# The last pass's up layer by seven products of eight, its down layer so in every second group, and two steps of the first pass placed later

## The chip, the cores and the metric

One core of a Trainium2 chip runs the whole kernel. The metric is the device time of one execution in microseconds; of the kernel before there are three runs, and their median is 2684.53 us. TensorE (PE) multiplies matrices out of SBUF into PSUM, which has eight banks here called by number; VectorE (DVE), ScalarE (ACT) and GpSimd (POOL) do the elementwise work; SyncE (SP) issues most of the transfers. Each engine works off its own queue in order.

## The reference

One layer of an encoder on 2048 tokens of width 1024, then a norm. What the change touches is the last third:

```python
h = h + xo @ w_xo[l]                                   # cross-attention, 256 memory tokens

u = rmsnorm(h, norm_mlp_g[l]) @ w_up[l]                # 1024 -> 4096
h = h + jnp.square(jax.nn.relu(u)) @ w_down[l]         # 4096 -> 1024
return rmsnorm(h, norm_final_g)
```

Before it stand a mixer (dilated window attention in eight heads, beside a convolution) with its out-projection, and cross-attention.

## The kernel before

**Passes.** The tokens are worked off in four passes of 512 (`post(p)`, p from 0 to 3; the last is `NG - 1`). A pass does the out-projection, cross-attention in two matrix products (`xs`, the scores; `x`, the probabilities times `bscr`), the norm, the MLP's up layer and its down layer. The attention of pass p + 1 and its convolution are woven into the instructions of pass p by generators, so the last pass runs alone. `first` is the attention of pass 0; its last steps are woven into the out-projection of pass 0.

**Precision.** Every fp32 operand is split into two fp16 halves, a high one (ScalarE copies) and a low one (VectorE subtracts). `mm3` then makes one product of three matmuls: high by high, high by low, low by high.

**The MLP.** The 4096 hidden features are eight groups `fg` of 512. A group has an up layer (1024 x 512 weights, 96 matmuls of 512 columns or as many halves) and a down layer (512 x 1024). In pass 0 the weights are split and stored (`wst`); later passes load the halves. Loaded weights lie in seven rotating tiles (`wtile`).

**Seven products of eight.** A product of matrices in 2 x 2 blocks can be made by seven block products instead of eight, with sums of blocks before and after. `prep` makes the seven weight blocks of the up layer for all eight groups in passes 1 and 2 and stores them (`ust`). `quad` is the up layer of one group by them: the normed tokens are needed as blocks B11, T1, T4, B2 and T32, which `columns` and `put` make in place of the plain halves `y`, and 7 x 24 matmuls of 256 columns run in four steps. In `quad`, `kept` copies a product from PSUM, `done` adds one, multiplies by the norm's factors `rsb`, squares, and splits the result into the halves `hh`. Pass 1 uses `quad` for groups 5 to 7, pass 2 for all, pass 3 for none.

**The last pass before.** `last_mlp` uses the plain up layer (`hidden`, four tiles of 128 features a group). The down layer of groups 0 to 6 is by seven products (`seven`): the raw fp32 weights are loaded as four quarters, VectorE makes four differences of them (`sums` and one more), seven pieces are split into halves (`piece`, a tile of 128 x 1024 each), and `parts` makes the blocks of the hidden features: A11, A12, A22 and the sums S1 to S4. The result is added into rows of tokens (`row`), which `to_rows` turns from columns first. X, Y and Z are pairs of PSUM banks; X takes the products A11, S2, S3 and A22 in turn, and VectorE reads it after each. The last group is plain, and each 128 tokens are normed and written as they are done.

**Order.** The program's order isn't a queue's order. A scheduler orders each engine's queue by a model of times of its own: an instruction goes when it is ready in that model, the earlier one in the program first. `after(...)` and `pinned(...)` hold an instruction behind the last one noted on the same engine. In `combine`, the results of a pair of heads are put together: the loads `ld`, then the sums `csm` (line 1162), the exponentials, the products, a transposition into `cath` and `catl`, which the out-projection needs. In `post`, the norm before the MLP is `rstd_from` (sums on TensorE `nps`, line 1466, then a power on GpSimd and three small steps on VectorE) and `bcast_rows` (four transpositions `nrb`, line 355) into `rsb`.

Of the kernel before, what the change touches and what calls it, by code (L numbers as in the profile page):

```python
# [21 lines left out]
P = 128  # L22
# [26 lines left out]
def hybrid_layer(ctx, tc, A, out):  # L49
# [1576 lines left out]
    def quad(p, fg, src, hh, rsb):  # L1626
# [21 lines left out]
        def done(e, pt, i, z):  # L1648
            DVE.tensor_tensor(e, e, pt, op=ALU.add)
            e3 = halved(e)  # L1650
            last["dve"] = DVE.scalar_tensor_tensor(e3, e3, 0.0, rsb[:, 256 * z:256 * z + 256].unsqueeze(1).to_broadcast([P, 2, 256]),
                                                   op0=ALU.max, op1=ALU.mult)
            ACT.activation(e, e, AF.Square)
            a, b = (t[:, 2 * i:2 * i + 2, 256 * z:256 * z + 256] for t in hh)
            ACT.copy(a, e3)
            DVE.tensor_tensor(b, e3, a, op=ALU.subtract)  # L1656

        X, Y, Z = (ps(f"u{x}", "up") for x in "xyz")
# [16 lines left out]
        Y = ps("uy", "up")  # L1675
# [8 lines left out]
    def post(p):  # L1684
# [10 lines left out]

        y = ytiles("y")
# [36 lines left out]
        for hp in range(XH // 2):  # L1733
# [21 lines left out]
        if p in preps:  # L1755
# [20 lines left out]
        if p == 2:  # L1776
            opened = hidden_tiles(0, order[0])
            opened = (opened, quad(p, order[0], src, opened, rsb))
# [4 lines left out]
        ACT.activation(rsb, rb, AF.Copy, scale=K_UP)  # L1783
# [3 lines left out]
        if p == NG - 1:  # L1787
            last_mlp(hs, y, rsb)
            return
        for g in range(FG // 2):  # L1790
# [3 lines left out]
            for i, fg in enumerate(fgs):  # L1794
# [6 lines left out]
                if src and (p == 2 or fg > 4):  # L1801
                    while fg not in ready:
                        next(prepping[p])
                    yield from main_quad or quad(p, fg, src, ht, rsb)
                    ks = (0, 1, 2, 3, 6, 7, 4, 5)
                    continue
                for c in range(4):
# [9 lines left out]
                    r = tmp("rl")  # L1817
                    last["dve"] = DVE.scalar_tensor_tensor(r, pt, 0.0, rsb, op0=ALU.max, op1=ALU.mult)
                    ACT.activation(r, r, AF.Square)
                    j = 4 * i + c  # L1820
                    last["act"] = ACT.copy(hh["h", j], r)  # L1821
                    DVE.tensor_tensor(hh["l", j], r, hh["h", j], op=ALU.subtract)
# [41 lines left out]
    def last_mlp(hs, y, rsb):  # L1864


        FG, p = 8, NG - 1
        banks.update(up=(4, 5, 6, 7), ux=(0, 1), uy=(2, 3), tr=(0, 1, 2, 3))
        acc = [xp_.tile([P, 4, 512], F32, tag=f"x{q}0", name=f"rows{q}") for q in "hl"]
        grow = [wk.tile([P, 512], F32, tag="sm", name=f"gain_row{c}", bufs=3) for c in range(2)]  # L1870
        for c in range(2):
            dma(grow[c], A["norm_final_g"][512 * c:512 * c + 512].unsqueeze(0).to_broadcast([P, 512]))

# [16 lines left out]
        def hidden(fg, c):  # L1890

            wh, wl = wpost(wcols(w_up, fg * 512 + c * P), f"u{p}{fg}_{c}", S_UP, (P, 8, P), 4 * fg + c, p)
            pt = ps("up", "up")
            for k in range(KC):
                mm3(pt, wh[:, k, :], wl[:, k, :], y["h", k], y["l", k], k == 0, k == KC - 1)
                if fg == 0 and c < 2 and k % 2:
                    to_rows(4 * c + k // 2)
            r = tmp("rl") if c else cv.tile([P, 512], F32, tag="vr", name="rl", bufs=2)
            last["dve"] = DVE.scalar_tensor_tensor(r, pt, 0.0, rsb, op0=ALU.max, op1=ALU.mult)
            ACT.activation(r, r, AF.Square)  # L1900
            return r

        def halves(x):
            return x.rearrange("p (j t) -> p j t", j=2)

        q1 = [xquad(q, 1, f"hq{q}") for q in "hl"]
        z1 = [[zp.tile([P, 512], F16, tag=f"z{3 * i + n}", name=f"hz{i}{n}") for n in range(3)] for i in range(2)]
        A1, S3 = ([halves(x[:, n]) for x in q1] for n in range(2))
        A2 = [x[:, 2:4] for x in q1]
        S12, S4 = [x[0:2] for x in z1], [halves(x[2]) for x in z1]  # L1910

        def parts(rs_, c):
            r, j = rs_[c], c % 2
            lo, hi = r[:, 0:256], r[:, 256:512]
            if c < 2:
                split([x[:, j] for x in A1], lo)
                DVE.tensor_tensor(lo, lo, hi, op=ALU.subtract)
                split([x[:, j] for x in S3], lo)
            else:
                r0 = rs_[j]  # L1920
                split([x[:, j] for x in A2], r)
                DVE.tensor_tensor(r0[:, 256:512], r0[:, 256:512], hi, op=ALU.add)
                DVE.tensor_tensor(r0[:, 0:256], hi, r0[:, 0:256], op=ALU.subtract)
                split([x[j] for x in S12], r0)
                DVE.tensor_tensor(lo, lo, r0[:, 0:256], op=ALU.subtract)
                split([x[:, j] for x in S4], lo)
# [19 lines left out]
        def piece(w, name):  # L1946
            return two(split_to(wtile(name, 4, (P, 2, 512)), w, S_DN))

        def sums(b):

            for o, x, y_ in ((b[0, 0], b[0, 1], b[0, 0]), (b[4], b[1, 1], b[0, 0]), (b[0, 1], b[1, 1], b[0, 1])):
                DVE.tensor_tensor(o, x, y_, op=ALU.subtract)

        def seven(fg, b, first):
            left, right = slice(0, 256), slice(256, 512)
            half = {"A11": A1, "S3": S3, "S4": S4, "A12": [x[:, :, left] for x in A2], "A22": [x[:, :, right] for x in A2]}
            at = {k: (lambda x, j, t, k=k: half[k][x][:, j, P * t:P * t + P]) for k in half}
            at["S2"] = lambda x, j, t: S12[x][j][:, P * t:P * t + P]
            at["S1"] = lambda x, j, t: S12[x][j][:, 256 + P * t:256 + P * t + P]
            X, Y, Z = ([ps(kind, "dn") for _ in range(2)] for kind in ("ux", "uy", "uy"))  # L1960
            for n, (key, w, pts, more, t0, c0) in enumerate((
                    ("A11", b[0, 0], X, False, 0, 0), ("A12", b[1, 0], Y, False, 0, 0),
                    ("S2", b[4], X, True, 0, 1), ("S1", b[0, 0], Z, False, 2, 1),
                    ("S3", b[0, 1], X, True, 2, 1), ("S4", b[1, 1], Z, True, 0, 1),
                    ("A22", b[1, 0], X, True, 2, 0))):
                wh, wl = piece(w, f"d{p}{fg}_{n}") if n else first
                if n == 1:
                    DVE.tensor_tensor(b[1, 0], b[1, 0], b[4], op=ALU.subtract)
                for t in range(2):
# [4 lines left out]
                    last["dve"] = DVE.scalar_tensor_tensor(a, pts[t], K_DN, a, op0=ALU.mult, op1=ALU.add)  # L1974

        rs_ = []
        for fg in range(FG - 1):
            b = {4: room(4, "b")}
            for c in range(4):
                if c or not fg:  # L1980
                    rs_.append(hidden(fg, c))
                for h in range(2) if 0 < c < 3 else ():
                    b[c - 1, h] = quarter(fg, c - 1, h)
                if c == 3:
# [109 lines left out]
```

## Time and profile before

| | us |
|---|---|
| three runs, median (lowest to highest) | 2684.53 (2680.31 to 2685.0) |
| the profiled execution, its own time | 2687.11 |
| its span | 2685.3 |
| its mean granted clock of TensorE | 0.992 |
| bytes read and written in HBM | 376.6 and 131.5 MB |
| last pass, first matmul of the out-projection about | 2222 |
| first matmul of the last pass's up layer | 2357.3 |

A group's row in the profile reads: line, engine, operation, the tile written and those read, their shapes, how many; then busy time, the mean of one in ns, and the idle time of the engine before them with what ended it. A timeline's row begins with start and duration. A row of waits reads: who waited, for whom, total, times, longest.

### The profile page before, as it was taken

The numbers are of one execution on the slowest core, as the hardware profiler recorded it, in microseconds if no ns is written. First come the engines' busy times: TensorE is split into PE (matmuls) and PEld (weight loads), VectorE is DVE, ScalarE is ACT, GpSimd is POOL, SyncE is SP. The second block draws the span as 40 slices with busy tenths as digits, with TensorE's granted clock in tenths as the row PEclk, the third lists the DMA queues.
The fourth block names the chain that finished last, engine by engine and source line by source line (L and its number), as shares of the span: only waits on it lengthen the run. The fifth ranks groups of instructions, "written<-read, shape, count | busy, mean of one in ns | idle before, by whom it ended". The sixth has DMA issues, their size and how long they took to land.

```text
span 2685.3 us, 43789 instructions
## 1 busy us (share of the span) xinstructions
PE 2613.5 (97%) x16786; PEld 1561.7 (58%) x16786; DVE 1982.5 (74%) x3816; ACT 1245.2 (46%) x2189; POOL 226.2 (8%) x285
## 2 busy tenths in 40 slices
PE   8999999999899999999999999999999999999998
PEld 7844448766454555445576676555776565444443
DVE  5886656567679996556799985468999755677976
ACT  5637544476454345334552343256443343443433
POOL 1234002132001011100000000000000000000000
PEclk9999999999999999999999999999999999999999
DMA  9977978665526777855357777454787765323331
GB/s 270 296 259 215 286 227 268 176 194 169 164 85 180 231 218 217 267 183 166 118 161 227 216 233 235 126 159 124 234 272 255 232 227 157 102 71 102 114 114 63
DMA packets 445634, 510.97 MB, mean 190 GB/s; under 512 B 89613, under 2 KB 341441, under 8 KB 444656
## 3 DMA queue, kind: packets, MB, share of 16 engines
q1 hardware_dynamic: 438016, 493.15, 60.1%
q10 hardware_dynamic: 5184, 9.01, 0.9%
q0 software_dynamic: 2224, 6.01, 0.6%
q8 instruction: 132, 2.16, 0.3%
q14 instruction: 78, 0.64, 0.1%
HBM read 376.59 MB, written 131.48 MB: 189 GB/s over the span
## 4 chain that ended last, share of the span: by engine, by line
PE 75%; DVE 12%; DMA 6%; issue 3%; ACT 3%; SPq 1%; POOL 1%; DVEq 0%; POOLq 0%; ACTq 0%
PE dn L376 7%; PE dn L375 7%; PE dn L374 7%; PE up L374 6%; PE up L376 6%; PE up L375 6%; PE lin L376 3%; PE lin L374 3%; PE lin L375 3%; DVE cacc L391 3%; PE xs L375 2%; PE xs L376 2%; PE xs L374 2%; PE pt L1030 2%; PE x L375 2%
## 5 line engine op out<-in xcount | busy, mean ns | idle before, releaser
L391 DVE SCALAR_TENSOR_TENSOR cacc<-cu,cw,cacc 128x512 f32<-128x512 f32 x480 | 365.8, 768 | 5.0
L375 PE MATMUL dn<-hhl,ws_d 128*128 128x512 f16 x768 | 291.6, 380 | 1.4 <-DVE hhl L1656 1.1
L376 PE MATMUL dn<-hhh,ws_d 128*128 128x512 f16 x768 | 291.6, 380 | 0.0
L374 PE MATMUL dn<-hhh,ws_d 128*128 128x512 f16 x768 | 288.9, 380 | 1.0 <-ACT hhh L1821 0.4
L374 PE MATMUL up<-mh,ws_u 128*128 128x512 f16 x512 | 194.1, 380 | 0.9 <-ACT mh L1509 0.9
L375 PE MATMUL up<-ml,ws_u 128*128 128x512 f16 x512 | 194.5, 380 | 0.0
L376 PE MATMUL up<-mh,ws_u 128*128 128x512 f16 x512 | 194.4, 380 | 0.0
L1024 ACT ACTIVATE sm<-sm,o 128x256 f32<-128x256 f32 (+1 forms) x288 | 119.4, 455 | 130.7 <-DVE o L1023 130.2
L1023 DVE CUSTOM_DVE_ANT_0 sm<-s,mask,qks 128x256 f32<-128x256 f32 (+1 forms) x384 | 151.9, 436 | 34.4 <-PE s L1064 33.7
L1034 DVE TENSOR_TENSOR pl<-pt,ph 128x512 f16<-128x512 f32 x160 | 110.1, 688 | 41.2 <-ACT ph L1033 40.5
L1838 DVE SCALAR_TENSOR_TENSOR h<-dn,bd,h 128x512 f32<-128x512 f32 x96 | 71.7, 749 | 78.6 <-PE dn L376 76.9
L376 PEld LDWEIGHTS <-ws_d 128*128 128x128 f16 x768 | 75.3, 98 | 90.9 <-issue 2.1
L1033 ACT CAST ph<-pt 128x512 f16<-128x512 f32 x160 | 91.4, 572 | 77.7 <-PE pt L1030 77.5
L375 PEld LDWEIGHTS <-ws_d 128*128 128x128 f16 x768 | 75.2, 98 | 83.3 <-issue 0.8
L374 PEld LDWEIGHTS <-ws_d 128*128 128x128 f16 x768 | 75.3, 98 | 82.6 <-issue 0.7
L376 PEld LDWEIGHTS <-ws_u 128*128 128x128 f16 x832 | 81.7, 98 | 64.0 <-issue 0.6
L375 PEld LDWEIGHTS <-ws_u 128*128 128x128 f16 x832 | 81.6, 98 | 61.6 <-issue 0.9
L374 PEld LDWEIGHTS <-ws_u 128*128 128x128 f16 x832 | 81.6, 98 | 60.9 <-issue 0.6
L1030 PE MATMUL pt<-ident,sm 128*128 128x128 f32 x640 | 99.4, 277 | 9.0 <-DVE catl L1200 4.2
L376 PE MATMUL o<-cath,ws_o 128*128 128x512 f16 x256 | 97.3, 383 | 4.8 <-DVE ws_o L362 4.8
L1030 PEld LDWEIGHTS pt<-ident,sm 128*128 128x128 f32 x640 | 79.2, 143 | 35.0 <-ACT sm L1024 4.2
L374 PE MATMUL o<-cath,ws_o 128*128 128x512 f16 x256 | 97.3, 382 | 0.8 <-ACT cath L1199 0.7
(556 smaller groups left out, 7296.4 us busy)
## 6 DMA issues: line engine op xcount, KB each, us to landing
ws_t<-ust SPq DMA_DIRECT2D x77, 512.0 KB
ws_d<-wst SPq DMA_DIRECT2D x64, 512.0 KB
ws_u<-wst SPq DMA_DIRECT2D x52, 512.0 KB
ust<-pt SPq DMA_DIRECT2D x48, 512.0 KB
raw_d<-in_w_down_dram SPq DMA_DIRECT2D x36, 512.0 KB
scan<-in_w_up_dram SPq DMA_DIRECT2D x32, 512.0 KB
scan<-in_w_down_dram SPq DMA_DIRECT2D x32, 512.0 KB
raw_o<-in_w_out_dram SPq DMA_DIRECT2D x32, 512.0 KB
```

The costliest lines, as they stand in the source:

```text
L374: PE.matmul(o, lh, rh, start=first, stop=False, skip_group_check=more)
L375: PE.matmul(o, lh, rl, start=False, stop=False, skip_group_check=more)
L376: last["pe"] = PE.matmul(o, ll, rh, start=False, stop=end, skip_group_check=more)
L391: DVE.scalar_tensor_tensor(acc, u[:, t:t + 512], cw[:, c, t:t + 1], acc, op0=ALU.mult, op1=ALU.add)
L1023: last["dve"] = DVE.tensor_tensor_reduce(dst, so, mask[:, 256 * m:256 * m + nk], SCORE, 3e38, ALU.add, ALU.min, mn)
L1024: last["act"] = ACT.activation(dst, dst, AF.Exp, bias=mn, scale=-1.0)
L1030: last["pe"] = PE.transpose(pt[:, j, :], sm[:, j, :], ident)
L1033: ACT.copy(ph, pt)
L1034: DVE.tensor_tensor(pl, pt, ph, op=ALU.subtract)
L1838: last["dve"] = DVE.scalar_tensor_tensor(hs[m], pt, K_DN, hs[m], op0=ALU.mult, op1=ALU.add)
```

## The change

In the last pass, the up layer is made by `quad` in all eight groups, with `ust` as in pass 2; so `columns` and `put` serve pass 3 too. The down layer is by seven products in groups 0, 2, 4 and 6, and plain in groups 1, 3, 5 and 7, with the stored halves of `wst` and matmuls of 256 columns. `quad` takes a `sink` for its results: `into` splits them into `hh` as before, and `blocks` makes A11 to S4 of them.

`last_mlp` becomes a generator that starts with the pass: it loads the quarters of group 0 at the head of the pass, makes their differences and first four pieces during the scores of the second pair of heads, and starts the first `quad` ahead of the norm. The pieces of a group by seven products lie in four tiles of the pool of `cath` and `catl`, are made ahead one step after each tile of the plain group before it (`steps_ahead`), and the last three inside `seven`. Each group's down layer runs behind the first step of the next group's up layer.

In pass 0, the combination of the last pair starts three empty steps later. In passes 0 and 1, `norm` runs in two parts behind the first and second tile of the up layer, and these two tiles are finished together.

```diff
@@ combine
         if end:
             ld = lds[p, pr]
+            for _ in range(3):
+                yield
@@ post
+        env = {}
+        mlp = last_mlp(hs, env) if p == NG - 1 else None
+        if mlp:
+            next(mlp)
...
                         late.append((pth, ptl, t, soft(sps[t], t)))
+                if mlp and hp:
+                    next(mlp)
                 yield
...
-        if p in preps:
+        if p:
             one, two_, src = columns(p)
...
-        r = rstd_from(ssum)
-        rb = ps("c", "nrb")
-        bcast_rows(rb, r, 4)
-        ACT.activation(rsb, rb, AF.Copy, scale=K_UP)
+        elif mlp:
+            env.update(src=src, rsb=rsb)
+            next(mlp)
+
+        def norm(step, st={}):
+
+            if step == 0:
+                st[0] = rstd_from(ssum)
+            elif step == 1:
+                rb = ps("c", "nrb")
+                bcast_rows(rb, st[0], 4)
+                ACT.activation(rsb, rb, AF.Copy, scale=K_UP)
+
+        held = None if p > 1 else []
+        if held is None:
+            norm(0)
+            norm(1)
...
+                    if held is None:
+                        finish(pt, 4 * i + c)
+                    else:
+                        norm(len(held))
+                        held.append((pt, c))
+                        if len(held) == 2:
+                            for a in held:
+                                finish(*a)
+                            held = None
@@ last_mlp
+            def sink(e, i, z):
+                q[i, z] = e
+                if z == i or i:
+                    split({(0, 0): A1, (1, 1): A22, (1, 0): A12}[i, z], halved(e))
+                    return
+                DVE.tensor_tensor(q[0, 0], q[0, 0], e, op=ALU.subtract)
+                DVE.tensor_tensor(e, e, q[1, 1], op=ALU.add)
+                DVE.tensor_tensor(q[1, 1], q[1, 1], q[0, 0], op=ALU.subtract)
+                split(S2, halved(q[1, 1]))
+                split(S1, halved(e))
+                DVE.tensor_tensor(q[1, 0], q[1, 0], q[1, 1], op=ALU.subtract)
+                split(S3, halved(q[0, 0]))
+                split(S4, halved(q[1, 0]))
...
+            q = [piece(n, w) for n, w in enumerate(((0, 0), (1, 0), 4, (0, 0), (0, 1), (1, 1), (1, 0)))]
+            return [q[0], sub((0, 0), (0, 1), (0, 0)), sub(4, (1, 1), (0, 0)), sub((0, 1), (1, 1), (0, 1)), q[1],
+                    sub((1, 0), (1, 0), 4), q[2], q[3]], q[4:]
...
+        def plain(fg, todo):
+
+            ws = [wpost(wcols(w_down, m * 256, 256, (4 * fg, 4 * fg + 4)), f"d{p}{fg}_{m}", S_DN, (P, 4, 256),
+                        32 + 4 * fg + m, p) for m in range(4)]
+            for t in range(4):
+                for c in range(2):
+                    pt = ps("tr", "dn")
+                    for h in range(2):
+                        wh, wl = ws[2 * c + h]
+                        for k in range(4):
+                            mm3(halved(pt)[:, h], *(x[:, k, P * t:P * t + P] for x in q1), wh[:, k], wl[:, k],
+                                not (h or k), k == 3, bool(h))
...
+                    if todo:
+                        todo.pop(0)()
...
+        ws = {}
+        nb = down_blocks(0)
+        yield
+        todo, late = steps_ahead(0, nb, ws)
+        for n, x in enumerate(todo):
+            x()
+            if n % 2:
+                yield
+        banks.update(qx=(4,), qy=(7, 5), qz=(6,), ux=(0, 1), uy=(2, 3), tr=(0, 1, 2, 3))
...
+        gen = blocks(0)
+        next(gen)
+        yield
+        for n in range(8):
+            to_rows(n)
+            if n % 2 and n < 7:
+                next(gen)
         for fg in range(FG - 1):
...
+            if fg % 2:
+                ws, todo = {}, []
+                if fg < FG - 2:
+                    todo, late = steps_ahead(fg + 1, nb, ws)
+                gen = blocks(fg + 1)
+            else:
+                gen = quad(p, fg + 1, env["src"], into(q1), rsb)
+            next(gen)
+            if fg % 2:
+                drain(plain(fg, todo))
+            else:
+                seven(fg, ws, late)
+                if fg < FG - 2:
+                    nb = down_blocks(fg + 2)
+            for _ in range(3):
+                next(gen)
         ss = top.tile([P, 8], F32, tag="fin", name="fin")
+        for t, c, a in plain(FG - 1, []):
+            ACT.activation(tmp("sq"), a, AF.Square, accum_out=ss[:, 2 * t + c:2 * t + c + 1])
```

More of the change, by code (lines that the diff above doesn't have):

```diff
@@ L1653, in done @@
             ACT.activation(e, e, AF.Square)
[L1654 to L1658, printed above, removed]
+            sink(e, i, z)
+        X, Y, Z = (ps(f"{'q' if p == NG - 1 else 'u'}{x}", "up") for x in "xyz")
         w11, w12 = pair(0)
@@ L1674, in quad @@
         done(e4, X, 1, 1)
-        Y = ps("uy", "up")
+        Y = ps("qy" if p == NG - 1 else "uy", "up")
         prod(Y, w22, "T4")
@@ L1862, in post, with last_mlp @@
             yield
-    def last_mlp(hs, y, rsb):
+    def last_mlp(hs, env):
         FG, p = 8, NG - 1
[L1868 to L1872, printed above, removed]
         def row(t):
@@ L1888, in split @@
             DVE.tensor_tensor(t[1], src, t[0], op=ALU.subtract)
[L1890 to L1926, printed above, removed]
+        def blocks(fg):
+            q = {}
+            def sink(e, i, z):
+                q[i, z] = e
[10 more added lines that the diff above has]
+                split(S4, halved(q[1, 0]))
+            return quad(p, fg, env["src"], sink, rsb)
@@ L1944, in quarter, with down_blocks @@
             return t
[L1946 to L1956, printed above, removed]
+        def down_blocks(fg):
+            return {4: room(4, "b"), **{(z, h): quarter(fg, z, h) for z in range(2) for h in range(2)}}
@@ L1974, in seven @@
                     last["dve"] = DVE.scalar_tensor_tensor(a, pts[t], K_DN, a, op0=ALU.mult, op1=ALU.add)
-        rs_ = []
-        for fg in range(FG - 1):
[L1978 to L1984, printed above, removed]
-                    first = piece(b[0, 0], f"d{p}{fg}_0")
-                    sums(b)
-                parts(rs_, c)
-            rs_ = [hidden(fg + 1, 0)]
-            seven(fg, b, first)
@@ L1990, in last_mlp @@
[L1990 to L2006 removed]
+                if n < 3:
+                    more_[n]()
```

81 lines of the change are left out of this document (45 added, 36 removed).

## The prediction

> **What bounds the kernel.** I read the first lines of the page, then the table of stages for the last pass, then what TensorE waited for. All times below are microseconds of the one profiled execution.
>
> ```profile
> span 2685.3 us, 43789 instructions
> PE 2613.5 (97%) x16786; PEld 1561.7 (58%) x16786; DVE 1982.5 (74%) x3816; ACT 1245.2 (46%) x2189; POOL 226.2 (8%) x285
> ```
>
> TensorE is busy for 97% of the span. The stages tell whether this holds where the change is. In the next fence the columns are the stretch, its length, busy time of each engine with its count of instructions, the granted clock, the DMA share and GB/s. Rows one to four are the last pass: the scores, cross-attention's second product, the MLP up to its last group, that group's down layer and the end; the last row is the MLP of the pass before, which uses the seven-product up layer already.
>
> ```profile
> 2270.40:2311.60 41.20, 41.15 (x204) 20.16 (x203) 21.93 (x45) 15.43 (x30) 1.01 (x1) 1.00 0.31 98
> 2311.60:2357.30 45.70, 44.04 (x211) 20.65 (x210) 27.14 (x45) 20.66 (x38) 0.00 (x0) 1.00 0.27 85
> 2357.30:2641.00 283.70, 282.69 (x1330) 130.47 (x1329) 229.21 (x334) 109.37 (x158) 1.01 (x1) 1.00 0.32 100
> 2641.00:2685.30 44.30, 36.37 (x169) 16.27 (x167) 24.85 (x49) 14.33 (x27) 2.21 (x4) 0.97 0.17 63
> 1870.00:2222.00 352.00, 346.65 (x2611) 239.51 (x2610) 294.96 (x546) 142.93 (x242) 3.77 (x5) 1.00 0.73 236
> ```
>
> In the MLP of the last pass TensorE is idle for 1.0 of 283.7 at full clock, while VectorE has 229.2 of work: the bound is TensorE, and VectorE is the second. DMA moves 100 GB/s there, less than half of what the pass before sustained. So a matmul less in this stage is time less, as long as VectorE and the loads keep behind cover.
>
> **The matmuls, term one.** A matmul's own 0.38 us overlaps with the next; what counts is the distance of two starts. I take it from an unbroken run of each width.
>
> ```profile
> 2399.33 0.38 PE L374 MATMUL dn<-ws_d,hz 128*128 128x512 f16 x1
> ...
> 2401.70 0.38 PE L376 MATMUL dn<-ws_d,hz 128*128 128x512 f16 x1
> ```
>
> ```profile
> 2149.83 0.27 PE L374 MATMUL up<-T1h,ws_t 128*128 128x256 f16 x1
> ...
> 2153.43 0.27 PE L376 MATMUL up<-T32h,ws_t 128*128 128x256 f16 x1
> ```
>
> Twelve of 512 columns start within 2.37, so 2.37/11 = 0.2155 each; thirty-four of 256 columns start within 3.60, so 3.60/33 = 0.1091 each. Two halves cost 0.2182, 1% more than a whole. Counts of before, one of the three lines of `mm3` each:
>
> ```profile
> L374 PE MATMUL up<-mh,ws_u 128*128 128x512 f16 x256 | 96.5, 379 | 0.0
> L374 PE MATMUL dn<-ws_d,hqh 128*128 128x512 f16 x112 | 42.0, 379 | 0.2 <-DVE rowsh L1974 0.2
> L374 PE MATMUL dn<-ws_d,hz 128*128 128x512 f16 x84 | 31.8, 379 | 0.3 <-ACT hz L1887 0.3
> L374 PE MATMUL dn<-ws_d,hhh 128*128 128x512 f16 x32 | 11.8, 379 | 0.0
> ```
>
> Up layer: before 3 x 256 = 768 wide ones, 165.5. After, eight groups of seven products of 24 halves, 1344 x 0.1091 = 146.6. That is -18.9. Down layer: before 3 x (112 + 84 + 32) = 684 wide ones, 147.4: seven groups by seven products and one plain. After, four groups of 84 wide ones, 72.4, and four plain groups of 192 halves, 83.8, together 156.2. That is +8.8. **TensorE has 10.1 less.** Norm, row transposes and the out-projection keep their counts.
>
> **VectorE's cover, term two.** The rows are those that the changed groups are made of: weight pieces, their differences, the adds into the rows, the up layer's end; then, from the pass before, the seven-product up layer's.
>
> ```profile
> L362 DVE SCALAR_TENSOR_TENSOR ws_d<-b,bd,ws_d 128x1024 f16<-128x1024 f32 x41 | 52.6, 1284 | 8.9 <-ACT ws_d L361 8.9
> L361 ACT ACTIVATE ws_d<-b,bd 128x1024 f16<-128x1024 f32 x41 | 47.0, 1147 | 57.1 <-PE dn L376 46.6 <-PE up L376 7.7 <-DMA b<-in_w_down_dram 2.6
> L1952 DVE TENSOR_TENSOR b<-b,b 128x1024 f32<-128x1024 f32 x14 | 17.1, 1221 | 0.0
> L1974 DVE SCALAR_TENSOR_TENSOR rowsh<-dn,bd,rowsh 128x512 f32<-128x512 f32 x56 | 40.9, 750 | 7.8 <-PE dn L376 7.8
> L1899 DVE SCALAR_TENSOR_TENSOR rl<-up,ssumx 128x512 f32<-128x512 f32 x32 | 21.7, 688 | 19.1 <-PE up L376 14.6 <-ACT ssumx L1783 4.5
> L1922 DVE TENSOR_TENSOR rl<-rl 128x256 f32<-128x256 f32 x14 | 5.9, 422 | 1.1 <-ACT rl L1900 1.1
> ```
>
> ```profile
> L1656 DVE TENSOR_TENSOR hhl<-e,hhh 128x512 f16<-128x512 f32 x32 | 22.1, 690 | 3.2 <-ACT hhh L1655 3.1
> L1651 DVE SCALAR_TENSOR_TENSOR e<-e,ssumx 128x512 f32<-128x512 f32 x32 | 22.0, 690 | 3.4 <-ACT ssumx L1783 3.4
> L1649 DVE TENSOR_TENSOR e<-e,up 128x512 f32<-128x512 f32 x32 | 21.8, 685 | 3.4 <-ACT e L1645 2.4 <-PE up L376 1.0
> L1653 ACT ACTIVATE e<-e 128x512 f32<-128x512 f32 x32 | 20.1, 628 | 34.6 <-DVE e L1651 34.5
> L1655 ACT CAST hhh<-e 128x512 f16<-128x512 f32 x32 | 19.6, 617 | 0.6
> ```
>
> Before, a group by seven products: 4 x 0.688 for the up layer, 14 halves and differences of 256 columns at 0.42 and 4 of 512 at 0.69 (8.6), 7 pieces at 1.284, 4 differences at 1.221, 14 adds at 0.750: 35.7 for TensorE's (96 + 84) x 0.2155 = 38.8. After, two groups together: up layers 8 x (0.685 + 0.690) = 11.0; halves 4 + 7 at 0.690 and 4 differences of 512 columns, which I take like L1649, 10.3; pieces 9.0; their differences 4.9; adds (14 + 8) x 0.750 = 16.5. That is 51.7 for 2 x 168 x 0.1091 + 18.1 + 21.0 = 75.7 of TensorE. VectorE's share falls from 92% to 68% by the same count, so on the mean it isn't the bound. Loads: 22 transfers (14 for the two up layers, 4 plain, 4 raw) of the size of this row, 11.5 MB in 75.7, 152 GB/s against the 236 that the pass before held.
>
> ```profile
> ws_t<-ust SPq DMA_DIRECT2D x77, 512.0 KB
> ```
>
> What is local needs its own look. The operand S2 stands behind a chain after the last up product: 0.685 + 0.690, ACT 0.628, three differences at 0.69, ACT 0.617, 0.690: 5.4. Ahead of its use lie step 0 of the next up group, 48 x 0.1091 = 5.2, and two down products, 24 x 0.2155 = 5.2. Cover 10.4, slack 5.0, and VectorE has in that stretch and the five products after it 1.4 + 5.5 + 10.5 + 3 x 1.284 = 21.2 of work in 5.2 + 18.1 = 23.3. Priced at nothing if VectorE's queue is in that order; without cover it is the slower rival. While TensorE waits for S2, the four later products, the next up group's and its loads wait behind it. Bounds on all waits inside the loop: -1.0 (the 1.0 that is idle before goes) and, by rival C, +20. Nearest is the pass before, whose MLP with this up layer and more load lost 352.0 - 346.65 = 5.35 over eight groups, attention's waits among them. I take +1.0 for new waits and -1.0 for the old ones.
>
> The plain last group has no product of a next group ahead of it. Its third operand hangs on e3's chain, 0.685 + 0.690 + 0.628 + 0.617 + 0.690 = 3.3 and the passing on between engines, against 24 x 0.1091 = 2.6 and two operand pairs, 0.7. I take +1.0 (0 to 2). Before, `hidden` of the last group covered it.
>
> **Entry of the MLP, term three.** `put` replaces the plain halves of the normed rows. For m of 4 to 7 it has, beside the 0.75 of the residual and 0.69 of the sum, these four forms and two more halves of 256 columns at 0.42:
>
> ```profile
> L1614 DVE SCALAR_TENSOR_TENSOR t<-h,gxm,t 128x256 f32<-128x256 f32 x4 | 1.9, 484 | 0.1
> L1613 DVE SCALAR_TENSOR_TENSOR t<-h,gxm,yv 128x256 f32<-128x256 f32 x4 | 1.9, 482 | 0.5 <-ACT yv L1612 0.5
> L1618 DVE TENSOR_TENSOR T32l<-t,T32h 128x512 f16<-128x512 f32 x4 | 2.8, 688 | 0.0
> ```
>
> Together 0.75 + 0.48 + 0.48 + 0.69 + 0.69 + 0.42 + 0.42 + 0.69 = 4.6, with a weight piece 5.9, against 24 x 0.2155 = 5.2 of TensorE: up to 0.7 late per tile, 2.8 over the four. (For m under 4 it is 0.75 + 0.69 + 0.42 + 2 x 0.48 = 2.8, less than the 5.2.) The product of B21 needs the last tile 0.75 + 0.62 + 0.48 + 0.48 + 0.62 + 0.69, some 4 with the passing on, after its last matmul (ScalarE's two copies taken like L1655); before it stand B11's 24 halves, 2.6, three operand pairs, 1.0, and row transposes that are ready. +0.7 (0 to 3). The norm is asked for only behind that, and its four transposes wait behind two more products; priced at nothing.
>
> `steps_ahead(0)` adds 4 x 1.284 + 4 x 1.221 = 10.0 to VectorE during the scores, where it has 41.2 - 21.9 = 19.3 idle, and 4.6 to ScalarE. Its four tiles come free when the out-projection ends. What is late next is the probabilities, which TensorE already waits for:
>
> ```profile
> PE ptx L1727 <- DVE ptl L1730: 1.0, 1, 1.0
> PE x L374 <- ACT pth L1729: 0.7, 1, 0.7
> ```
>
> +1.0 (0 to 5, one piece or two in front of the soft-max). The four raw loads for it stand at the head of SP's queue of this pass, ahead of the out-projection's weights; their rooms were attention's, which the program has ended by then, so they hold nothing up: 0, or the time of one transfer.
>
> **The first pass, term four.** Two waits there cost more than they show, for the clock falls behind them. The fences are VectorE's timeline (start, duration, engine, line), two rows of waits, and stretches with the columns of the table of stages.
>
> ```profile
> 685.71 0.17 DVE L1162 TENSOR_TENSOR csm<-ld 128x8 f32<-128x8 f32 x1 [5.13 <-issue]
> ...
> 686.22 1.28 DVE L362 SCALAR_TENSOR_TENSOR ws_o<-raw_o,bd,ws_o 128x1024 f16<-128x1024 f32 x1
> ```
>
> ```profile
> PE o L376 <- DVE ws_o L362: 4.8, 1, 4.8
> ...
> PE nrb L355 <- DVE nr L350: 2.5, 1, 2.5
> ```
>
> ```profile
> 685.00:690.00 5.00, 2.44 (x6) 0.87 (x7) 4.29 (x12) 1.13 (x3) 0.00 (x0) 0.57 1.05 270
> 690.00:695.00 5.00, 5.00 (x33) 2.95 (x32) 1.88 (x7) 1.49 (x3) 0.00 (x0) 0.74 0.74 205
> 1586.00:1590.00 4.00, 2.06 (x25) 1.58 (x24) 4.00 (x10) 2.94 (x5) 0.00 (x0) 1.00 0.96 254
> 1590.00:1594.00 4.00, 4.00 (x15) 1.69 (x14) 4.00 (x8) 1.92 (x5) 0.00 (x0) 0.57 0.55 218
> ```
>
> The combination of the last pair (L1162) stood in VectorE's queue ahead of a weight piece, and both waited for a load: 4.8 on TensorE, and 5 x 0.43 + 5 x 0.26 = 3.4 by the clock; 8.2 if it goes whole. The three empty steps put the combination later in the program. But the queue's order is the scheduler's, which took L1162 before a piece that the program has earlier, so it goes by readiness as it models it, and what L1162 is ordered behind (`after`, the last scores) is the same after as before. I expect the place in the queue, and the wait, to stay: 0, bounds -8.2 and +3 (a later transposition of the pair holds the out-projection's last part). `norm` behind two tiles: before, three tiles of the up layer ran ahead of these transposes already, as many as there are banks, and the sums' products were late by VectorE's queue, which the edit doesn't shorten. 0, bounds -7 and +4. In the second pass likewise.
>
> **The sum.** -10.1 - 1.0 + 1.0 + 1.0 + 0.7 + 1.0 = -7.4. The profiled execution took 2687.11 (span 2685.3 and 1.8 around it), 2.6 over the median of 2684.53. So 2679.7 for such an execution and 2677.1 for the median: **2677**. Its own range is 2672 to 2682.
>
> **A rule on the clock.** In the rows of 1586 to 1594, 1.94 of idle time is enough: the clock is at 0.57 in the 4 behind it. The Trainium skill ("TensorE: Matmul & The Clock Gate", "What's actually happening") says that the array falls to half its clock after an idle window of some 3.4 us; by that, rival C below would cost its waits alone, 4 x 3.3, and end at 2690 as an estimate. By the rows each wait costs 1.7 more (4 x 0.43), and I go by them.
>
> **The rivals.** A: the first pass's wait goes too. For it, a later place in the program may be a later place in the queue; against it, the order argued above. -7.4 - 8.2: 2669. B: new waits give most back, without the loop: two pieces in front of the soft-max, +4 over what I took, and B21 late by +2.3: 2683, about the same. C, slower: S2. If the scheduler puts adds and pieces ahead of the chain, VectorE is late by more than the slack of 5.0, in each of four groups. At 3.3 of wait and 1.7 of clock, 4 x 5.0 = 20: 2697. It decides from 1.8 per group on, 7.4/4. For it, 21.2 of 23.3 is tight and the chain crosses engines four times; against it, 92% of VectorE before left 1.0 of waits in seven such groups. That the work isn't less is excluded by the counts.
>
> **How the numbers follow.** The forecast 0.50, A 0.18, B 0.14, C 0.18. 0.2% is 5.4 us, about what a measurement of this kernel tells from no change: faster is below 2679.2, slower above 2689.9. Faster: four fifths of the forecast and A, 0.58. Slower: C and the ends of the others, 0.21. Same: 0.21. The range goes from 2666, 3 under A, to 2693, which leaves out half of C and little else.
>
> **What would show it.** Right: in the last pass 1344 halves named up, 336 wide and 768 half ones named dn, TensorE idle under 4 in the MLP, VectorE near 70% of it; L1162 in the first pass still waiting ahead of a weight piece. Wrong: TensorE waiting for the halves of S2 or S1, or for a piece `ws_d` of a group by seven products; the clock under 1.00 anywhere behind 2311; or a first pass shorter by 8.

## The result and the profile after

The changed kernel takes 2675.08 us, the median of seven runs (2672.52 to 2675.94), beside 2684.53 before (seven runs, 2680.31 to 2687.46). The ratio is 0.9965 with a 95% interval of 0.9954 to 0.9977: faster by 9.45 us. The prediction was 2677 and "faster". The profiled execution took 2675.08, its span is 2673.3; that of before took 2687.11. So the two profiles differ by 12.0, and it is this number that the traces have to explain. Of the runs further down, one of the four of `written_twelve` is slow (3059.81 at a granted clock of 0.844) and left out of its median and ratio. First the page of the kernel after:

```profile
span 2673.3 us, 45710 instructions
PE 2602.2 (97%) x17782; PEld 1660.2 (62%) x17782; DVE 1942.8 (73%) x3751; ACT 1236.1 (46%) x2182; POOL 226.4 (8%) x285
```

The table of stages of after, with the columns used before: scores, cross-attention's second product, the MLP up to its last group, the end.

```profile
2270.40:2311.50 41.10, 41.04 (x203) 20.07 (x202) 29.11 (x52) 18.15 (x34) 1.01 (x1) 1.00 0.36 110
2311.50:2357.10 45.60, 43.93 (x211) 20.61 (x209) 33.84 (x67) 25.21 (x50) 0.00 (x0) 1.00 0.29 98
2357.10:2629.00 271.90, 271.90 (x2186) 214.18 (x2185) 174.34 (x239) 94.26 (x138) 1.01 (x1) 1.00 0.46 146
2629.00:2673.30 44.30, 36.24 (x310) 30.05 (x307) 23.99 (x51) 10.69 (x24) 2.21 (x4) 0.94 0.20 72
```

The scores and the second product take what they took (41.1 and 45.6), although VectorE has 7.2 and 6.7 more to do in them. The MLP is shorter by 11.8; TensorE is never idle in it, the loads went from 100 to 146 GB/s, and VectorE from 229.2 of 283.7 (81%) to 174.3 of 271.9 (64%). What TensorE waits for from the scores to the end of after is two rows, two of the five of before; the other three of before stand in the fence behind them:

```profile
PE ptx L1740 <- DVE ptl L1743: 1.0, 1, 1.0
PE x L374 <- ACT pth L1742: 0.7, 1, 0.7
```

```profile
PE dn L376 <- DVE hz L1888: 0.5, 1, 0.5
PE dn L374 <- ACT hz L1887: 0.3, 1, 0.3
PE dn L374 <- DVE rowsh L1974: 0.2, 1, 0.2
```

The matmuls of after's MLP, one of the three lines of `mm3` each (plain groups, then those by seven products, then one operand of the up layer):

```profile
L374 PE MATMUL dn<-ws_d,hqh 128*128 128x256 f16 x256 | 69.5, 273 | 0.0
L374 PE MATMUL dn<-ws_d,hqh 128*128 128x512 f16 x64 | 24.3, 379 | 0.0
L374 PE MATMUL dn<-ws_d,hz 128*128 128x512 f16 x48 | 18.2, 379 | 0.0
L374 PE MATMUL up<-T32h,ws_t 128*128 128x256 f16 x128 | 34.9, 273 | 0.0
```

3 x 256 halves and 3 x (64 + 48) = 336 wide ones: the predicted counts. The span from the first start of this MLP's up layer to the last start of its down layer is the measure for all that follows, called **the last stage**. Of before and of after, the first and the last matmul in it:

```profile
2357.26 0.38 PE L374 MATMUL up<-mh,ws_u 128*128 128x512 f16 x1
...
2676.99 0.38 PE L376 MATMUL dn<-ws_d,hhl 128*128 128x512 f16 x1
```

```profile
2357.26 0.27 PE L374 MATMUL up<-B11h,ws_t 128*128 128x256 f16 x1
...
2664.97 0.27 PE L376 MATMUL dn<-ws_d,hql 128*128 128x256 f16 x1
```

319.73 and 307.71, and both start at the same moment: the difference of the two profiles, 12.0, is in this stage whole. Ahead of it, the way from the first matmul of the last pass's out-projection (2222.27 in both) is 134.99 in both.

### The profile page after: what moved, and what is told of

Same layout as the page of the kernel before. It is cut to its first block, busy times and chain, and to the rows that moved or that the text cites. A ratio compares the mean times of both kernels' runs of the same rounds, so it can differ in the third digit from the quotient of the medians.

```text
span 2673.3 us, 45710 instructions
## 1 busy us (share of the span) xinstructions
PE 2602.2 (97%) x17782; PEld 1660.2 (62%) x17782; DVE 1942.8 (73%) x3751; ACT 1236.1 (46%) x2182; POOL 226.4 (8%) x285
## 5 line engine op out<-in xcount | busy, mean ns | idle before, releaser
L375 PEld LDWEIGHTS <-ws_t 128*128 128x128 f16 x1064 | 104.3, 98 | 23.2 <-issue 9.5
L374 PEld LDWEIGHTS <-ws_t 128*128 128x128 f16 x1064 | 104.5, 98 | 15.0
L376 PEld LDWEIGHTS <-ws_t 128*128 128x128 f16 x1064 | 104.4, 98 | 14.1
L374 PE MATMUL x<-pth,ws_b 128*128 128x512 f16 x256 | 95.7, 379 | 2.3 <-ACT pth L1742 1.2
L375 PE MATMUL o<-catl,ws_o 128*128 128x512 f16 x256 | 97.8, 382 | 0.0
L375 PE MATMUL up<-ml,ws_u 128*128 128x512 f16 x256 | 97.5, 381 | 0.3 <-DVE ml L1512 0.3
```

What stands on the lines that cost most here:

```text
L374: PE.matmul(o, lh, rh, start=first, stop=False, skip_group_check=more)
L375: PE.matmul(o, lh, rl, start=False, stop=False, skip_group_check=more)
L376: last["pe"] = PE.matmul(o, ll, rh, start=False, stop=end, skip_group_check=more)
```

## The experiments

All medians stand beside before on the same chip (2683.69 for the first four runs, 2682.81 for the next four, 2684.60 for the last three).

| run | median | ratio to before, 95% interval | last stage |
|---|---|---|---|
| mlp_alone | 2672.36 | 0.9954 (0.9942 to 0.9967) | 307.71 |
| first_alone | 2683.15 | 0.9999 (0.9991 to 1.0008) | 319.73 |
| s2_twelve | 2670.13 | 0.9955 (0.9940 to 0.9970) | 307.71 |
| seven_all | 2664.12 | 0.9930 (0.9915 to 0.9946) | 299.22 |
| written | 2673.84 | 0.9965 (0.9952 to 0.9979) | 308.40 |
| written_twelve | 2723.82 | 1.0158 (1.0143 to 1.0174) | 359.92 |
| piece_first | 2665.53 | 0.9937 (0.9925 to 0.9950) | 307.71 |
| nr_pool | 2672.38 | 0.9957 (0.9944 to 0.9969) | 307.71 |
| after_again | 2671.67 | 0.9958 (0.9943 to 0.9973) | 307.71 |
| both | 2657.69 | 0.9901 (0.9885 to 0.9917) | 299.22 |
| three | 2654.57 | 0.9884 (0.9867 to 0.9901) | 299.22 |

The last stage comes out the same to 0.01 us wherever its instructions are the same. What varies from execution to execution is the time ahead of it: its start lies between 2352.8 and 2357.3 in the profiles of before, of after and of the first four runs. That before and after start it at the same moment is chance.

### Which part of the change carries the gain

```diff
 mlp_alone, against after:
-            for _ in range(3):
-                yield
-        held = None if p > 1 else []
+        held = None
```

> The changed kernel without its two edits of the first passes: the last pair's combination at its old place in the program, the norm ahead of the layer's first tiles again; the last pass as changed. Theory (all of the gain is in the last pass): -9 to -10 us against before, median 2675, the span before the last pass's up layer as in both traces (2357.1 to 2357.3). Rival (the two edits of the first passes give 2 to 4 of the 9.45, hidden in the run-to-run spread of the one profile): 2677 to 2679.

> The kernel before with only the two edits of the first passes. Theory: 0, within 1.5 us of before, with L1164-like csm<-ld still ahead of the weight piece in VectorE's queue and TensorE's wait for that piece at 4.6 to 4.8. Rival: -2 to -4 (the edits carry a part of the gain), or the -8.2 that the wait and the clock behind it would be worth if the combination did move.

> The changed kernel unaltered, beside the same runs of before as the two kernels below. Theory (the gain is the last stage's 320.11 to 307.98, and what differs besides lies in the first 2350 us from run to run): a ratio of 0.9955, -12 us. Rival (the two edits of the first passes cost 2 to 3 us, for without them the median was 2672.36 and with them 2675.08): a ratio of 0.9965, -9.5.

The new last pass alone gives 0.9954, the whole change 0.9965 and, the second time, 0.9958, the two other edits alone 0.9999. The intervals of the first three overlap, and the last stage is the same, so the two edits neither give nor cost anything that these runs can tell. In first_alone, the waits and VectorE's queue of the first pass:

```profile
PE o L376 <- DVE ws_o L362: 5.1, 1, 5.1
...
PE nrb L355 <- DVE nr L350: 2.8, 1, 2.8
```

```profile
686.42 0.17 DVE L1164 TENSOR_TENSOR csm<-ld 128x8 f32<-128x8 f32 x1 [4.30 <-issue]
...
686.93 1.27 DVE L362 SCALAR_TENSOR_TENSOR ws_o<-raw_o,bd,ws_o 128x1024 f16<-128x1024 f32 x1
```

Three empty steps later in the program, the combination still stands ahead of the weight piece, and the norm's transposes still wait.

### How much cover the operand S2 has

```diff
 s2_twelve, against after:
+                for _ in range(12):
+                    DVE.tensor_tensor(q[1, 1], q[1, 1], q[1, 1], op=ALU.max)
                 split(S2, halved(q[1, 1]))
```

> The changed kernel with the chain ahead of the operand S2 made longer: twelve extra VectorE operations (each the maximum of the block with itself, 128x512, 0.69 us, which leaves the values as they are) between the third difference and the split into halves, 8.3 us more in each of the four groups by seven products. The prediction's slack for this chain is 5.0. Theory: TensorE is late by 8.3 - 5.0 = 3.3 in each of four groups, and its clock falls behind each wait (1.7): +13 to +20, 2688 to 2695 against the changed kernel's 2675, with TensorE's waits at dn<-hz or dn<-S2 halves. Rival 1 (the slack is much larger, for the scheduler finds other work to put ahead): under +4. Rival 2 (the slack was nearly gone already and only luck hid it): each us of the 8.3 shows, +33, 2708.

Nothing is lost: the last stage is 307.71 again, so the theory failed and rival 1 came. After's own trace shows why a slack counted in the written order is not the slack there is. ScalarE's high half of S2 first, which waits for the third difference (L1934), then VectorE's low halves of S1 and of S2, then TensorE around them:

```profile
2461.60 0.62 ACT L1920 CAST hz<-e 128x512 f16<-128x512 f32 x1 [0.64 <-DVE e L1934]
```

```profile
2461.48 0.68 DVE L1921 TENSOR_TENSOR hz<-e,hz 128x512 f16<-128x512 f32 x1
...
2463.28 0.68 DVE L1921 TENSOR_TENSOR hz<-e,hz 128x512 f16<-128x512 f32 x1
```

```profile
2466.31 0.38 PE L376 MATMUL dn<-ws_d,hql 128*128 128x512 f16 x1
2466.53 0.27 PE L374 MATMUL up<-T32h,ws_t 128*128 128x256 f16 x1
...
2467.62 0.27 PE L375 MATMUL up<-T32l,ws_t 128*128 128x256 f16 x1
2467.73 0.38 PE L374 MATMUL dn<-ws_d,hz 128*128 128x512 f16 x1
```

The low half at 2461.48 was begun before that high half was there, so it is S1's; S2's is ready at 2463.96 (an expectation below puts it at 2462.07). In the written order the third matmul of its product would need it at 2466.53 + 2 x 0.2155 = 2466.96: 3.0 of slack. The high half, ready at 2462.22, would be needed at 2466.53: 4.3. But between the second and the third lower product, and again further on, stand halves of the *next* up group. The program's scheduler put them there, and in s2_twelve it put four whole up products and the product of S1 ahead of S2's. So I fixed TensorE's order to the written one, without and with the twelve operations:

```diff
 written, against after (`written` is empty until the head of the last pass's MLP loop):
+        with ExitStack() as st:
+            after(st, *written)
             PE.matmul(o, lh, rh, ...)
             PE.matmul(o, lh, rl, ...)
             last["pe"] = PE.matmul(o, ll, rh, ...)
...
+        written.append("pe")
```

> The changed kernel with TensorE's order in the last pass's MLP fixed to the order in which the program writes it: each product issued behind the one before. (In the changed kernel the scheduler puts products of the next up group between the seven lower products.) Theory (the written order alone has cover, as the prediction reckoned it: S2's halves are ready at 2462.07 in the trace of the changed kernel and the two products ahead of it end at 2466.44, 4.4 of slack): the stage from the first up product to the last lower one stays at 308.0, at most +1 for each group by seven, so within 0 to +4 of the changed kernel. Rival (the free order is what hides the chain): each of the four groups late by 2 to 5, +8 to +20.

> As the run before, and with the twelve extra VectorE operations (8.3 us) ahead of S2's halves that cost nothing when the scheduler ordered TensorE freely. Theory (the slack in written order is 4.4 to 5.0 and the free order made it elastic): 3.3 to 3.9 of wait in each of four groups, 0.16 more each for the modelled ends, and up to 1.7 of slower clock behind each: +14 to +23, a stage of 322 to 331 where the changed kernel has 308.0. Rival (the order does not matter, VectorE hides the twelve in any order): 308 to 310.

In written order the change as it is loses 0.7, at one place. TensorE's waits in its last stage, then those with the twelve, then stretches of one of the four groups with the twelve:

```profile
PE dn L378 <- DVE hql L1635: 0.5, 1, 0.5
```

```profile
PE dn L376 <- ACT hz L1922: 41.1, 4, 10.6
PE dn L378 <- DVE hql L1635: 0.5, 1, 0.5
```

```profile
2475.00:2480.00 5.00, 0.48 (x3) 0.00 (x0) 4.96 (x7) 1.15 (x1) 0.00 (x0) 1.00 0.29 105
2480.00:2485.00 5.00, 0.00 (x0) 0.00 (x0) 4.76 (x8) 0.00 (x0) 0.00 (x0) 0.59 0.34 105
2485.00:2490.00 5.00, 3.89 (x10) 1.37 (x11) 3.19 (x5) 1.24 (x2) 0.00 (x0) 0.50 0.00 0
2490.00:2495.00 5.00, 5.00 (x22) 2.14 (x21) 3.21 (x4) 1.15 (x1) 0.00 (x0) 0.89 0.03 3
```

For `written` the theory held. For `written_twelve` theory and rival both missed: +51.5 against `written`, 12.9 for each group, where 5.8 were expected at most (3.9 + 0.16 + 1.7). VectorE's queue of that group tells where the rest is from (L1938 are the extra operations):

```profile
2471.47 0.68 DVE L1938 TENSOR_TENSOR e<-e 128x512 f32<-128x512 f32 x1
2472.08 0.74 DVE L1998 SCALAR_TENSOR_TENSOR rowsh<-dn,bd,rowsh 128x512 f32<-128x512 f32 x1
...
2474.60 1.27 DVE L362 SCALAR_TENSOR_TENSOR ws_d<-b,bd,ws_d 128x1024 f16<-128x1024 f32 x1
...
2478.91 6.49 DVE L1938 TENSOR_TENSOR e<-e 128x512 f32<-128x512 f32 x9
2485.43 0.69 DVE L1941 TENSOR_TENSOR e<-e,e 128x512 f32<-128x512 f32 x1
```

From the third difference, done at 2470.35, to the last extra operation, done at 2485.40, it is 15.05: the 8.3 of the twelve and, between them, the low half of S1, two steps of the up layer's end, four adds into the rows and two weight pieces. S2's high half would have been there at 2471.0, ScalarE's 0.6 behind the difference, and was wanted at 2475.3, so 15.05 less 4.3 is the wait. Behind it come some 2.4 of clock: 51.5 - 41.1 is 10.4 over four groups, 2.6 each, of which 0.16 is the modelled end. So the wait that the prediction feared exists, and is dear, where TensorE's order leaves it nothing else to take.

### More groups by seven products

```diff
 seven_all, against after (the loop over the groups):
-            if fg % 2: ...
+            gen = blocks(fg + 1) if fg < FG - 2 else quad(p, fg + 1, env["src"], into(q1), rsb)
+            next(gen)
+            seven(fg, ws, late)
+            todo, ws = [], {}
+            if fg < FG - 2:
+                todo, late = steps_ahead(fg + 1, down_blocks(fg + 1), ws)
+            for n in range(3):
+                next(gen)
+                for x in todo[3 * n:3 * n + 3]:
+                    x()
```

> The changed kernel with the lower layer by seven products in all of the first seven groups of the last pass, not in every second one. Theory (TensorE bounds this stage and VectorE at 64% has room): each of the three groups more takes 84 wide products, 18.1 us, in place of 192 half ones, 20.95: -2.85 three times, -8.5 against the changed kernel, 2666.5; VectorE rises from 174 us of 272 to some 225 of 263. Rival (weights late): the raw quarters can only be loaded once the group before has used its own, so loads, differences and pieces must fit in the 26 us from the fourth product to the next group's first; if they are late by 4 us in each of six groups, the gain is gone and the time is 2675 plus 6 x 4 - 8.5 + clock, 2690 or more, with TensorE waiting for ws_d. VectorE's own queue late shows as waits for S2 (hz) instead.

The stage is 8.49 shorter, -8.55 was reckoned. The stretch of its MLP up to the last group:

```profile
2352.50:2616.00 263.50, 263.50 (x1867) 182.90 (x1865) 233.46 (x311) 119.82 (x167) 1.01 (x1) 1.00 0.47 150
```

VectorE has 233.5 of 263.5, 89%. TensorE still waits for nothing: the rival's waits for `ws_d` did not come. Every second group was not the limit.

### The waits of the first pass

```diff
 piece_first, against after:
-        DVE.scalar_tensor_tensor(t[:, 1], raw, ...)
+        last["piece"] = DVE.scalar_tensor_tensor(t[:, 1], raw, ...)
...
-            after(st, "dve")
+            after(st, "dve", *(["piece"] if end else []))
             DVE.tensor_tensor(mm_, ld[:, 0, ...
```

> The changed kernel with the last pair's combination of the first pass ordered behind the last weight piece ws_o in VectorE's queue, which the three empty steps were not able to do. Theory (TensorE's 4.6 there and the half clock behind it, 6.8 us at half, 3.4, are VectorE's queue): -8.0, near 2667, with no TensorE wait for ws_o near 682. Rival (what is late next: the chain of the combination still begins when its load lands at 685.2, and its transposition, now at 704.8, cannot come before some 702): TensorE, ahead by 8, waits there instead; -2 to -4, with a new wait of TensorE for cat or cath between 694 and 702.

VectorE's timeline there, and the stretches:

```profile
680.35 1.28 DVE L362 SCALAR_TENSOR_TENSOR ws_o<-raw_o,bd,ws_o 128x1024 f16<-128x1024 f32 x1
...
684.05 0.17 DVE L1164 TENSOR_TENSOR csm<-ld 128x8 f32<-128x8 f32 x1 [0.42 <-DMA ld<-oscr]
```

```profile
680.00:685.00 5.00, 4.35 (x30) 2.64 (x31) 4.48 (x12) 1.98 (x5) 0.00 (x0) 1.00 0.72 130
685.00:690.00 5.00, 5.00 (x45) 2.85 (x44) 3.20 (x16) 2.69 (x7) 0.95 (x2) 1.00 0.97 299
```

With the piece ahead, TensorE is idle for 0.65 of these ten and the clock stays whole (0.57 in 685 to 690 of the run before). From the first out-projection product to the first scores the trace has 45.7 (672.1 to 717.8) where after has 52.1 (673.3 to 725.5). In the ten traces without this edit the stretch is 51.4 to 53.8, in the three with it 45.7 to 46.0: 5.4 to 8.1 less. By the medians, the run is 8.3 under `written` of the same chip, whose stage costs 0.7 more than this one's, so 7.6, and 6.9 under `nr_pool`, of the same chip and with the same last stage. The rival's wait at the transposition did not come: TensorE waits 0.7 for `cath` there, as it does in after. The norm's wait was tried by itself:

```diff
 nr_pool, against after (in the norm of the first two passes, W is GpSimd):
+        if W:
+            W.tensor_tensor(t, dst, dst, op=ALU.mult)
+            W.tensor_tensor(t, t, v, op=ALU.mult)
+            W.tensor_scalar(t, t, -0.5, 1.5, op0=ALU.mult, op1=ALU.add)
+            W.tensor_tensor(dst, t, dst, op=ALU.mult)
+            return
```

> The changed kernel with the last three small steps of the norm's chain in the first two passes on GpSimd instead of VectorE, where pairs of 0.7 us operations stand between them (nps read at 847.6, nr done at 853.95). Theory (the wait of 2.8 before nrb is VectorE's queue, and the half clock at 855.8 for 6.8 us follows from it): nr done by some 851.5, the wait gone, the clock whole: -2.8 and -3.4, 2669. Rival 1 (only the wait goes, the clock falls anyway for the short waits around 856 to 860): -2.8. Rival 2 (GpSimd's small steps, 0.5 to 1.0 each in the trace, take as long as VectorE's queue did): 0.

The waits of nr_pool in that place, and VectorE's queue:

```profile
PE opt L1044 <- DVE o L1278: 2.7, 1, 2.7
PE nrb L361 <- POOL nr L352: 1.3, 1, 1.3
```

```profile
852.19 3.39 DVE L397 SCALAR_TENSOR_TENSOR cacc<-cu,cw,cacc 128x512 f32<-128x512 f32 x5
855.50 1.27 DVE L368 SCALAR_TENSOR_TENSOR ws_u<-raw_u,bd,ws_u 128x1024 f16<-128x1024 f32 x1
...
857.36 0.42 DVE L1278 COPY o<-opt 128x260 f32<-128x260 f32 x1
```

The norm's wait went from 2.8 to 1.3, and a new one of 2.7 stands behind it, for a copy out of attention's bank: between the last masked scores (`sm`) and this copy VectorE's queue has one weight piece and one convolution step (`cacc`) more than in after. 0.9957 against 0.9958: nothing gained, though none of the three expectations had this reason.

### The parts put together

```diff
 three, against both (both is seven_all and piece_first together):
-            for _ in range(2 if p else 6):
+            for _ in range((2, 5, 2)[p - 1] if p else 6):
```

> The lower layer by seven products in all seven groups of the last pass, and the last pair's combination of the first pass behind the weight piece in VectorE's queue. Theory (the two gains lie in different stages and add): -8.5 and -7 to -8.3 against the changed kernel, 2656 to 2659; the last stage 299.5. Rival (with the first pass shorter, loads of the later passes come into each other's way): 2662 or more.

> As the run before, and the combinations in the third group of attention (beside the second pass's layers) three steps further behind their load, where VectorE stands 5.5 to 7.9 us at csm<-ld and TensorE waits 5.5 to 6.8 for the halves of e. Theory (here more steps do move it in VectorE's queue, for its order has it behind the layer's own operations): the wait near 1640 goes, and with it some 3.4 us of half clock: -5 to -10 against the run before, some 2650. Rival (the combination ends later and the next pass's out-projection waits for cath, or another small wait takes its place): 0 to +4.

The two gains add, within what these runs can tell: `both` takes 2657.69, 1.0% under before and 14.0 under after_again, where 5.4 to 8.1 and the last stage's 8.5 make 13.9 to 16.6. In `three` the wait that was aimed at is gone and another has grown. TensorE's waits from 1570 to 1660 in both, then in three (1570 to 1600), then the clock in three:

```profile
PE up L374 <- ACT e L1656: 3.7, 1, 3.7
PE lps2m L411 <- DVE lsum L416: 1.0, 1, 1.0
```

```profile
PE lps2m L411 <- DVE lsum L416: 3.0, 1, 3.0
```

```profile
1580.00:1585.00 5.00, 2.05 (x19) 1.61 (x17) 3.52 (x6) 0.78 (x2) 0.00 (x0) 1.00 0.78 295
1585.00:1590.00 5.00, 5.00 (x30) 3.55 (x30) 5.00 (x12) 4.16 (x7) 0.00 (x0) 0.53 0.42 138
```

The intervals of the two overlap; that the three steps are worth anything is not shown.

## Why the prediction was right, and by how much it was off

- **The matmuls, -10.1.** Right. Summed over the starts in the trace, the up layer went from 165.8 to 146.7, and the down layer, its waits taken out, from 147.4 to 156.3: -10.2.
- **The old waits in the loop, -1.0.** Right in kind, too small. The starts of before's down layer stand 149.24 apart in all, 1.85 more than 683 x 0.2158 (the mean of its up layer, 165.76 / 768). The trace shows 1.0 of this as idle time, since it counts from a modelled end. One of the places, in before:

```profile
2627.39 0.38 PE L376 MATMUL dn<-ws_d,hz 128*128 128x512 f16 x1
2628.09 0.39 PE L374 MATMUL dn<-ws_d,hz 128*128 128x512 f16 x1 [0.31 <-ACT hz L1887]
```

The starts are 0.70 apart, 0.48 more than the 0.2155 of an unbroken run, and 0.31 is shown. So -10.2 - 1.85 = -12.0, which is the whole difference of the profiles. All five places stand between 2625.9 and 2633.2, in the one group whose 72 wide down products run without an up product between them (2621.0 to 2638.4; in the other groups by seven products 48 in a row at most).

- **The four allowances, +3.7.** This is the step that failed: new waits in the loop +1.0, the last plain group +1.0, the entry +0.7, the scores +1.0. None of them shows in after: the way to the last stage is 134.99 as before, and in the stage TensorE waits for nothing. `written` gives what two of them are in the order that the prediction reckoned with: no wait at S2, and 0.7 lost at the last plain group (its `hql` row). In the kernel as built even that is covered: the low half that `written` waits for is done 1.5 behind the first matmul of that layer in both runs, but the third low matmul needs it in `written`, while in after four of the layer start before it is done, put in front by the scheduler. The soft-max kept its two waits to the tenth, with 7.2 and 6.7 more of VectorE's work beside it.
- **The first pass, 0.** Right, with both reasons: L1164 kept its place, and the norm's wait stayed (2.5 before, 2.8 after). What rival A would have given, 8.2, is borne out by `piece_first` at about 7 (5.4 to 8.1); its condition, that a later place in the program is a later place in the queue, is not met.
- **The sum.** -7.4 for -12.0 between the profiles. Against the medians, 9.45 and in the second comparison 12.9, the prediction of 2677 was 2 to 5 too high, by the allowances and the 0.85 of the old waits. That the first median came within 2 of the forecast is luck: the last stage took off 12.0, and the time ahead of it, which moves by some 4 from run to run, hid a part.
- **Rival B** did not come: no wait before the soft-max or at the entry was added. **Rival C** is a real mechanism. Its slack was put at 5.0 and is 4.3 for the high half and 3.0 for the low one. Its price, 5.0 a group for 3.3 of wait, was not tried; `written_twelve`, whose chain is 8.3 longer, waits 10.3 and loses 12.9 a group, since a chain of VectorE's that grows lets other work of its queue in between. The point that it overlooked is that TensorE's order is the scheduler's in this pass, as VectorE's is, so that an operand that is late in the scheduler's model is met by moving products.
- **The rule on the clock.** In `three` a wait of 2.95 was enough for 0.53 of the clock in 1585 to 1590, as the 1.94 of idle time in the rows quoted ahead was for 0.57. The Trainium skill ("TensorE: Matmul & The Clock Gate", "What's actually happening") has the array fall after some 3.4 us idle; the measured wait is under that, so the rows were the better guide.
- VectorE's share came out at 64%, not near 70%, and never bounded the stage; in `seven_all` 89% does not either. The prediction's count adds up durations, and these overlap in the queue (0.68 long, 0.61 from start to start in the rows of `written_twelve`): for before it gave 92%, where the trace has 81%.
- **One sign of being wrong came,** the clock under 1.00 behind 2311: 0.94 in the last stretch, 0.97 in before. It says nothing, for in after it falls behind the last lower matmul (2664.97), in 2666.0 to 2673.3 (0.66), where TensorE has no work left.

## What to carry to other kernels

Where a scheduler orders the engines' queues, a slack counted in the order of the program is not the slack that the kernel has: look up what really stands between two dependent matmuls. Here products of the next layer moved in front, and 8.3 more of VectorE's work ahead of an operand cost nothing (`s2_twelve`), where the same in the written order cost 51.5. The twelve operations stood in the program, so the scheduler reckoned with them; a delay that its model does not know was not tried. The same freedom undoes edits: moving a step in the program did not move it in a queue (first_alone: 0.9999), while one explicit order behind the piece that the bound engine needs gave about 7 us. And the stage that TensorE bounds to 100% is summed up here from counts times the distance of starts alone, to 0.1 us (seven_all: -8.49 for -8.55).

## What the runs showed of the hardware

A wait of TensorE costs more than the idle time that the trace prints: for 512 columns up to 0.16 more each (0.38 of modelled length, 0.2155 between starts), which made 1.0 of shown idle 1.85 of lost time over five places. And the half clock behind a wait outlasts it: in `three` the wait ends at 1584.8, and the clock is at 0.53 in 1585 to 1590, when TensorE is busy throughout. Over the thirteen traces, between 160 and 2640 us, a stretch at half clock begins in or within 5 us behind each of the 40 idle times of TensorE of 2.3 us and more, 10 of the 14 of 1.94 to 1.99, and none of the 17 of 1.5 to 1.9, though three of 1.2 to 1.4 have one. It lasts 3.41 or 6.83 us, and 10.24 behind the four of over 9 us.
